# Last squares on VectorE, head transposes two steps later, a shorter Newton step in a two-block transformer kernel

## The chip, the cores and the metric

The kernel runs on one core of one Trainium2 chip. The core has five engines that work side by side, each from a queue of its own and in order: TensorE (PE, with PEld for its weight loads), VectorE (DVE), ScalarE (ACT), GpSimd (POOL) and SyncE (SP, which here only starts DMAs). The metric is device microseconds for one execution, the median of the timed runs.

## The reference

Two transformer blocks run one after the other on 256 tokens of width 2048, all in float32. The first has stick-breaking attention, sparse attention and a gated feed-forward; it ends in an RMS norm. The second, in which most of the change lies, has eight "Fox" heads (softmax attention with a forget bias) and eight "NSA" heads, which sum a compressed, a selected and a window branch, then a SwiGLU feed-forward:

```python
def _rms_norm(x, g):
    xf = x.astype(jnp.float32)
    y = xf * lax.rsqrt(jnp.mean(xf * xf, axis=-1, keepdims=True) + RMS_EPS)
    return (y * g.astype(jnp.float32)).astype(x.dtype)

def second_block(x, ...):
    h = _rms_norm(x, attn_norm[l])
    x = x + _hybrid_mixer(h, ...)     # o_fox and o_nsa, concatenated, @ w_out
    h = _rms_norm(x, ffn_norm[l])
    x = x + _swiglu(h, w_gate[l], w_up[l], w_down[l])

# in a head
    p = _masked_softmax(s, mask)      # exp(s - max) / sum
    o = jnp.einsum("bhqk,bkhd->bqhd", p, v)
```

With 256 tokens, all key blocks are selected and the window covers everything, so the kernel computes two softmax branches of 384 masked columns (128 for the first 128 queries, 256 for the others) in each NSA head, and one in each Fox head.

## The kernel before

**Main products.** Activations lie with features on partitions and tokens on the free axis. All weights are streamed: a piece of 128 rows by up to 1024 columns comes by DMA (`raw`), ACT rounds it into a high part (`wh`, L303), and DVE takes the difference as a low part (`wl`, L306). Each product is done as several passes over high and low parts (L344 to L365) into PSUM pool `pg` of four buffers. `run` goes over a list of items; before the products of one piece it emits the splitting of the piece three further on (`AHEAD`), so `wh` and `wl` (four buffers each) can run up to three pieces ahead of PE. A piece of two 128-row slices by 512 columns is 2.56 us of PE.

**Side work.** Attention heads and norms are generators in the list `active`. `spent` adds up the columns of the products emitted, and every 1.27 us of them (`TICK`) `tick` moves each generator to its next `yield`. So the place of side work in each engine's queue is fixed by counting ticks; the schedule is manual, and each engine takes its instructions in the order in which they were emitted. `wait(n)` lets n ticks go by. `drain(gens)` ticks until the named generators are done, with no main products between; a group's `pre` runs such a drain, after the splitting for its first piece was emitted. Tiles of one tag share a number of buffers; a new tile's first writer waits until all readers of the buffer's last tile are done. The small PSUM tiles (`psm`) come from `pm`, with four buffers, for scores, transposes, outputs and norm sums alike.

**Heads.** `nsa_head` (L1537): scores 1; scores 2 and the softmax of branch 1; then that of branch 2; each softmax writes p (tag `t2`, two buffers in the pool `mixt`) by L821 on DVE and its exponential on ACT (L210). Then both are scaled (L837 on DVE), `wait(W)` with W = 3, six transposes on PE (L843) into two `psm` tiles, copies to SBUF (L447 on ACT or L449 on DVE, by turns), `wait(W)`, and the products with V (L680). The output is split by L683 (ACT) and L685 (DVE), and that frees its `psm` tile. `nsa_chain` starts a head every 7 ticks (`seq`). `fox_head` (L1619) is the same with one p, a head every 5 ticks, and starts when the NSA heads are done. `drain([gens["fox"]])` stands as `pre` ahead of the second half of the output projection, which needs the Fox outputs.

**Norms.** `x_out` (L1106) runs for each of 16 feature tiles k: high part (ACT), low part (L1113, DVE), square (ACT, tile `sq` of two buffers), and the add of the square to the running sum (L1118, POOL). The first block's last down projection has two sums, the output projection of the second block one. A product with ones (L1303 and L1304, or L1190) sums over partitions, and `rsqrt_of` (L493) makes the reciprocal root by Ln and Exp and one Newton step on DVE. It is called five times: ahead of both mixers and both feed-forwards, and once for the norm between the blocks.

Of the kernel before, what the change touches and what calls it, by code (L numbers as in the profile page):

```python
# [12 lines left out]
OP = mybir.AluOpType  # L13
# [13 lines left out]
W = 3  # L27
# [97 lines left out]
def kernel(ctx: ExitStack, tc: tile.TileContext, t):  # L125
    nc = tc.nc
    out = t["out"]
# [76 lines left out]
    def lut(func, **kw):  # L204

        if func in (AF.Exp, AF.Ln):
            ln_exp()
        else:
            tables[0] = func
        nc.scalar.activation(func=func, **kw)  # L210
# [16 lines left out]
    def wait(n):  # L227
        for _ in range(n):
            yield
# [263 lines left out]
    def rsqrt_of(out_, src, inv_n, w):  # L493

        r0 = tmp.tile([128, T], F32, name="r0", tag="r0", bufs=1)[:, :w]
        m = tmp.tile([128, T], F32, name="mm", tag="mm", bufs=1)[:, :w]
        lut(out=r0, in_=src, func=AF.Ln, scale=inv_n, bias=epsc)
        lut(out=r0, in_=r0, func=AF.Exp, scale=-0.5)
        nc.vector.tensor_scalar(out=m, in0=src, scalar1=inv_n, scalar2=EPS, op0=OP.mult, op1=OP.add)
        nc.vector.tensor_mul(out=m, in0=m, in1=r0)  # L500
        nc.vector.tensor_mul(out=m, in0=m, in1=r0)
        nc.vector.tensor_scalar(out=m, in0=m, scalar1=-0.5, scalar2=1.5, op0=OP.mult, op1=OP.add)
        nc.vector.tensor_mul(out=out_, in0=r0, in1=m)

    def ident_rows(off):
        return lambda k: off + k
# [55 lines left out]
    def first_norm():  # L562
        rsqrt_of(rb, sqs[2][:, :T], 1.0 / D, T)
        keep_warm(WARM)
        h_scale(0)
# [498 lines left out]
    def xk(k):  # L1064
        return P["x"][k // 8][:, k % 8, :]
# [40 lines left out]
    def x_out(k, g_ap, pair, accs):  # L1106

        x = xk(k)
        hi, lo = pair(k)
        yield  # L1110
        nc.scalar.activation(out=hi, in_=x, func=AF.Identity, scale=g_ap)
        yield
        nc.vector.scalar_tensor_tensor(out=lo, in0=x, scalar=g_ap, in1=hi.bitcast(F32), op0=OP.mult, op1=OP.subtract)  # L1113
        for acc, sc in accs:
            sq = acc if k == 0 else P["late"].tile([128, T], F32, name="sq", tag="sq")
            nc.scalar.activation(out=sq, in_=x, func=AF.Square, scale=1.0 if sc is None else sc)
            if k:
                nc.gpsimd.tensor_tensor(out=acc, in0=acc, in1=sq, op=OP.add)  # L1118

    ssq = {}  # L1120

# [415 lines left out]
    def nsa_head(h):  # L1537
        g, qh = h // 4, R["qn"][:, h, :]
        sd = R["t"].tile([128, 384], F32, name="t1", tag="t1")
        nc.scalar.activation(out=sd, in_=C["dist"], func=AF.Copy, scale=2.0 ** -(h + 1))  # L1540
        yield
        S1 = scores(qh, R["kv"][:, 4 + g, :])
        yield
        S2 = scores(qh, R["kv"][:, 6 + g, :])
        p1, st1 = yield from softmax(S1, sd, R["t"])
        p2, st2 = yield from softmax(S2, sd, R["t"])
        for i, (p, st) in enumerate(((p1, st1), (p2, st2))):
            nc.vector.reciprocal(out=st[:, 0:2], in_=st[:, 4:6])
            nc.vector.tensor_mul(out=st[:, 0:2], in0=st[:, 0:2], in1=R["gat"][:, 1 + i, h, :])
            scale_rows(p, st[:, 0:2])  # L1550
        yield from wait(W)
        PT1 = transpose_p(p1)
        PT2 = transpose_p(p2)
        yield
        pT = []
        for PT in (PT1, PT2):
            x = R["t"].tile([128, 384], F32, name="t3", tag="t3", bufs=3)
            copy(x, PT[:, :384])
            pT.append(x)
        yield from wait(W)  # L1560
        j = h // 2
        vc = R["vcT"][32 * j:32 * j + 32, 128 * (h % 2):128 * (h % 2) + 128]
        yield from av_out(pT, [(R["vsw"], 128 * g), (R["vsw"], 256 + 128 * g)], oN(), h,
                          extra=(vc, R["pcT"][32 * j:32 * j + 32, :]))
# [54 lines left out]
    def fox_head(h):  # L1619
        cb = R["t"].tile([128, T], F32, name="cb", tag="cb")  # L1620
        s = R["scr"][h:h + 1, :]
        nc.scalar.dma_start(out=cb, in_=bass.AP(tensor=s.tensor, offset=s.offset, ap=[[0, 128], [1, T]]))
        yield
        yield
        cm = R["t"].tile([128, 384], F32, name="t1", tag="t1")
        nc.gpsimd.tensor_tensor(out=cm[:, 0:128], in0=cb[:, 0:128], in1=R["negc"][:, 0, 0:128], op=OP.add)
        nc.gpsimd.tensor_tensor(out=cm[:, 128:384], in0=cb, in1=R["negc"][:, 1, :], op=OP.add)
        S = scores(R["qf"][:, h, :], R["kf"][:, h, :])
        yield
        p, st = yield from softmax(S, cm, R["t"], R["cq"][:, :, h])  # L1630
        nc.vector.reciprocal(out=st[:, 0:2], in_=st[:, 4:6])
        scale_rows(p, st[:, 0:2])
        yield from wait(W)
        PT = transpose_p(p)
        yield
        pT = R["t"].tile([128, 384], F32, name="t3", tag="t3", bufs=3)
        copy(pT, PT[:, :384])
        yield from wait(W)
        yield from av_out(pT, [(R["vf"], 128 * h)], oF(), h)
# [125 lines left out]
```

## Time and profile before

| | |
|---|---|
| median of 3 runs | 2741.2 us (2741.12 to 2746.78) |
| profiled execution | 2742.96 us, of which the span 2741.2 us |
| PE busy | 2681.7 us, 98% |
| PE weight loads | 2344.1 us, 86% |
| DVE busy | 1961.9 us, 72% |
| ACT busy | 1353.8 us, 49% |
| POOL busy | 498.2 us, 18% |
| mean granted TensorE clock | 0.995 |

The span runs from the first to the last instruction. Times in rows are microseconds from its start. The second block's mixer lies at about 1558 to 2010.

### The profile page before, as it was taken

The page shows a single profiled execution, that of the slowest core. Times are in us where ns is not written, and L with a number is a line of the kernel's source. Part 1 is how long each engine was busy: PE and PEld are TensorE (multiplying, and loading weights), DVE is VectorE, ACT ScalarE, POOL GpSimd, SP SyncE. Part 2 cuts the span into 40 slices and gives each one's busy share as a digit, 9 for nine tenths or more (in the row PEclk, how much of TensorE's full clock was granted, in tenths as well). Part 3 has the DMA queues.
Part 4 walks back from the last instruction along what each step waited for, and adds up shares of the span by engine and source line. Part 5 has one row for each costly group of instructions (what it writes and reads, how often), then busy time and mean ns, then how long its engine had stood idle before and what let it go on. Part 6 is the DMA issues. An engine that isn't in the chain of part 4 may idle for free. (4 is left out here: it accounts for less than half of the span.)

```text
span 2741.2 us, 42225 instructions
## 1 busy us (share of the span) xinstructions
PE 2681.7 (98%) x16017; PEld 2344.1 (86%) x16017; DVE 1961.9 (72%) x2843; ACT 1353.8 (49%) x2022; POOL 498.2 (18%) x469
## 2 busy tenths in 40 slices
PE   8989999899999999999999999999999999999999
PEld 6879997788878888888888878888888888888888
DVE  8899877988877886556666756767876665556655
ACT  5544553444446555335555535555554554344543
POOL 0444310310512010000102301102222220012210
PEclk9999999999999999999999999999999999999999
DMA  9888757889876885566665675444566666666664
GB/s 358 263 273 305 231 191 226 268 292 321 303 246 198 300 300 186 185 194 190 193 189 187 194 218 158 152 131 154 169 187 194 190 190 192 189 189 191 191 196 144
DMA packets 303820, 591.16 MB, mean 216 GB/s; under 512 B 20980, under 2 KB 61020, under 8 KB 303486
## 3 DMA queue, kind: packets, MB, share of 16 engines
q1 hardware_dynamic: 299990, 583.61, 66.1%
q10 hardware_dynamic: 3626, 4.85, 0.8%
q8 instruction: 126, 2.06, 0.3%
q14 instruction: 78, 0.64, 0.1%
HBM read 582.54 MB, written 5.78 MB: 215 GB/s over the span
## 5 line engine op out<-in xcount | busy, mean ns | idle before, releaser
L348 PE MATMUL pg<-ring,wh 128*128 128x512 f32 x5408 | 1904.4, 393 | 1.1 <-DVE ring L1174 0.9
L306 DVE TENSOR_TENSOR wl<-raw,wh 128x1024 fp32r<-128x1024 f32 (+2 forms) x908 | 1141.1, 1269 | 616.9 <-ACT wh L303 606.1
L347 PE MATMUL pg<-ring,wl 128*128 128x256 f32 x5408 | 1524.0, 282 | 6.8 <-DVE wl L306 4.9
L303 ACT ACTIVATE wh<-raw 128x1024 fp32r<-128x1024 f32 (+2 forms) x908 | 928.9, 1039 | 878.2 <-PE pg L348 646.6
L348 PEld LDWEIGHTS pg<-ring,wh 128*128 128x128 f32 x5408 | 1019.4, 188 | 216.3 <-DVE ring L1174 3.3
L347 PEld LDWEIGHTS pg<-ring,wl 128*128 128x128 f32 x5408 | 1018.1, 188 | 36.0 <-issue 10.0
L482 POOL TENSOR_TENSOR ring<-gy,ring 128x256 fp32r<-128x256 f32 x88 | 110.2, 1262 | 749.4 <-ACT ring L480 749.4
L350 PE MATMUL pg<-ring,wh 128*128 128x256 f32 x672 | 190.5, 284 | 8.1 <-DVE ring L456 3.1
L352 PE MATMUL pg<-ring,wl 128*128 128x256 f32 x672 | 188.2, 280 | 6.2 <-DVE wl L306 6.1
L351 PE MATMUL pg<-ring,wh 128*128 128x256 f32 x672 | 188.8, 281 | 0.1
L344 PE MATMUL pg<-ring,wh 128*128 128x512 f32 x352 | 142.3, 404 | 5.3 <-DVE ring L456 2.0
L350 PEld LDWEIGHTS pg<-ring,wh 128*128 128x128 f32 x672 | 127.0, 189 | 11.5 <-DVE ring L456 3.4
L314 DVE CUSTOM_DVE_ANT_0 raw<-raw,cb,mod 128x1024 f32<-128x1024 f32 x96 | 135.3, 1409 | 1.2 <-DMA raw<-in_w_adaT 0.8
L352 PEld LDWEIGHTS pg<-ring,wl 128*128 128x128 f32 x672 | 126.9, 189 | 7.9 <-DVE wl L306 7.8
L314 DVE CUSTOM_DVE_ANT_0 raw<-raw,cb,vec 128x1024 f32<-128x1024 f32 x96 | 130.0, 1354 | 1.5 <-DMA cb<-cdram 1.5
L351 PEld LDWEIGHTS pg<-ring,wh 128*128 128x128 f32 x672 | 126.8, 189 | 0.9 <-DVE ring L600 0.3
L467 POOL TENSOR_TENSOR ring<-pt,ring 128x256 f32<-128x256 f32 x76 | 87.2, 1149 | 191.1 <-ACT pt L466 191.0
L1240 POOL TENSOR_TENSOR gy<-ga,rb 128x256 f32<-128x256 f32 x44 | 52.5, 1202 | 325.2 <-ACT ga L210 325.2
L345 PE MATMUL pg<-ring,wl 128*128 128x256 f32 x352 | 98.8, 281 | 0.0
L363 PE MATMUL pg<-wh,ring 128*128 128x512 f32 (+3 forms) x240 | 85.2, 355 | 0.0
L364 PE MATMUL pg<-wl,ring 128*128 128x512 f32 (+3 forms) x240 | 80.6, 336 | 0.3 <-DVE wl L306 0.3
L365 PE MATMUL pg<-wh,ring 128*128 128x512 f32 (+3 forms) x240 | 80.6, 336 | 0.0
(292 smaller groups left out, 2424.2 us busy)
## 6 DMA issues: line engine op xcount, KB each, us to landing
raw<-in_w_in SPq DMA_DIRECT2D x241, 512.0 KB, 4.7
raw<-in_w_adaT SPq DMA_DIRECT2D x192, 512.0 KB, 5.4
raw<-in_w_gate SPq DMA_DIRECT2D x176, 512.0 KB, 4.2
raw<-in_w_up SPq DMA_DIRECT2D x176, 512.0 KB, 4.2
raw<-in_w_down SPq DMA_DIRECT2D x176, 512.0 KB, 4.6
raw<-in_w_out SPq DMA_DIRECT2D x64, 512.0 KB, 5.7
raw<-in_w_o_sb SPq DMA_DIRECT2D x16, 512.0 KB, 5.1
raw<-in_w_o_dsa SPq DMA_DIRECT2D x16, 512.0 KB, 6.0
```

Of the source, the lines that this page charges most:

```text
L303: nc.scalar.activation(out=hi, in_=src, func=AF.Copy)
L306: nc.vector.tensor_sub(out=lo, in0=src, in1=hi.bitcast(F32))
L314: nc.vector.tensor_tensor_reduce(out=r, in0=r, in1=P["cb"][:, RAW * half:RAW * half + RAW], scale=1.0, scalar=below, op0=OP.mult, op1=OP.a ...
L344: nc.tensor.matmul(g.ps[f], hi[:, fs], both, start=True, stop=False)
L345: nc.tensor.matmul(ps, lo[:, fs], xh, start=False, stop=False)
L347: nc.tensor.matmul(ps, lo[:, fs], xh, start=False, stop=False)
L348: nc.tensor.matmul(g.ps[f], hi[:, fs], both, start=False, stop=stop)
L350: nc.tensor.matmul(ps, hi[:, fs], xh, start=start, stop=False)
L351: nc.tensor.matmul(ps, hi[:, fs], xl, start=False, stop=False)
L352: nc.tensor.matmul(ps, lo[:, fs], xh, start=False, stop=stop)
L467: nc.gpsimd.tensor_tensor(out=y, in0=x, in1=y, op=OP.add)
L482: nc.gpsimd.tensor_tensor(out=lo, in0=src, in1=hi.bitcast(F32), op=OP.subtract)
```

## The change

It has three parts. In `rsqrt_of` the Newton step after its first product is done by two `scalar_tensor_tensor` instructions instead of a product, a scale-and-add and a product: m(-0.5)r0, then (m + 1.5)r0. In `x_out` the adds of squares for k of 12 and more run on VectorE instead of GpSimd. In `nsa_head` and `fox_head` five ticks instead of three lie between the scaling of the probabilities and their transposes; `ds_head` of the first block keeps three.

```diff
@@ -498,9 +498,8 @@
         lut(out=r0, in_=r0, func=AF.Exp, scale=-0.5)
         nc.vector.tensor_scalar(out=m, in0=src, scalar1=inv_n, scalar2=EPS, op0=OP.mult, op1=OP.add)
         nc.vector.tensor_mul(out=m, in0=m, in1=r0)
-        nc.vector.tensor_mul(out=m, in0=m, in1=r0)
-        nc.vector.tensor_scalar(out=m, in0=m, scalar1=-0.5, scalar2=1.5, op0=OP.mult, op1=OP.add)
-        nc.vector.tensor_mul(out=out_, in0=r0, in1=m)
+        nc.vector.scalar_tensor_tensor(out=m, in0=m, scalar=-0.5, in1=r0, op0=OP.mult, op1=OP.mult)
+        nc.vector.scalar_tensor_tensor(out=out_, in0=m, scalar=1.5, in1=r0, op0=OP.add, op1=OP.mult)
@@ -1115,7 +1114,8 @@
             if k:
-                nc.gpsimd.tensor_tensor(out=acc, in0=acc, in1=sq, op=OP.add)
+                eng = nc.vector if k >= 12 else nc.gpsimd
+                eng.tensor_tensor(out=acc, in0=acc, in1=sq, op=OP.add)
@@ -1548,7 +1548,7 @@
             scale_rows(p, st[:, 0:2])
-        yield from wait(W)
+        yield from wait(W + 2)
         PT1 = transpose_p(p1)
         PT2 = transpose_p(p2)
@@ -1630,7 +1630,7 @@
         scale_rows(p, st[:, 0:2])
-        yield from wait(W)
+        yield from wait(W + 2)
         PT = transpose_p(p)
```

## Rows read from the trace of the kernel before

**Rows 1.** Page, part 1: busy us (share of span) and instructions of each engine.

```profile
PE 2681.7 (98%) x16017; PEld 2344.1 (86%) x16017; DVE 1961.9 (72%) x2843; ACT 1353.8 (49%) x2022; POOL 498.2 (18%) x469
```

**Rows 2.** Who waited for whom (total us, times, longest): PE, whole span; DVE, 1745 to 1960.

```profile
PE pm L843 <- DVE t L837: 6.1, 6, 2.2
...
PE pg L344 <- DVE ring L1174: 0.9, 1, 0.9
...
DVE t L821 <- PE pm L843: 1.4, 3, 0.7
```

**Rows 3.** Stretches: length; PE, PEld, DVE, ACT, POOL busy (instructions); PE clock; DMA.

```profile
1568.00:1573.00 5.00, 4.94 (x17) 3.96 (x18) 3.79 (x6) 3.75 (x5) 0.69 (x2) 0.66 0.74 239
...
1923.00:1928.00 5.00, 5.00 (x22) 4.32 (x21) 4.77 (x11) 1.64 (x4) 0.54 (x2) 0.66 0.95 325
...
1758.00:1763.00 5.00, 2.73 (x15) 1.83 (x15) 4.86 (x11) 3.28 (x6) 2.54 (x2) 1.00 0.36 107
```

**Rows 4.** Timeline of PE: start, us, instruction, [idle before it <- releaser]; transposes of two heads.

```profile
1761.54 0.70 PE L843 MATMUL pm<-con,t 128*128 128x128 f32 x3 [2.13 <-DVE t L837]
...
1922.48 0.70 PE L843 MATMUL pm<-con,t 128*128 128x128 f32 x3 [2.23 <-DVE t L837]
```

**Rows 5.** Timelines of DVE and PE around transposes of NSA heads 0, 1 and 2.

```profile
1763.46 0.28 DVE L821 CUSTOM_DVE_ANT_0 t<-pm,t 128x128 f32<-128x128 f32 x1
...
1777.19 0.42 DVE L685 TENSOR_TENSOR ring<-pm,ring 128x256 fp32r<-128x256 f32 x1
...
1777.75 0.46 PE L812 MATMUL pm<-ring 128*128 128x128 f32 x2 [0.21 <-DVE ring L685]
...
1792.62 0.82 PE L843 MATMUL pm<-con,t 128*128 128x128 f32 x6
...
1793.14 0.29 DVE L821 CUSTOM_DVE_ANT_0 t<-pm,t 128x128 f32<-128x128 f32 x1 [0.36 <-PE pm L843]
...
1793.36 0.42 DVE L821 CUSTOM_DVE_ANT_0 t<-pm,t 128x256 f32<-128x256 f32 x1
```

**Rows 6.** PE, end of Fox: main products of 1951.5 to 1956.47 by line, then timeline.

```profile
L348 PE MATMUL pg<-ring,wh 128*128 128x512 f32 x14 | 4.9, 393 | 0.0
...
1957.26 0.70 PE L843 MATMUL pm<-con,t 128*128 128x128 f32 x3
1958.74 0.94 PE L680 MATMUL pm<-t,ringv 128*128 128x128 f32 x6 [0.79 <-ACT t L447]
```

**Rows 7.** Timeline of DVE at the end of Fox.

```profile
1955.47 0.55 DVE L449 COPY t<-pm 128x384 f32<-128x384 f32 x1
...
1956.72 0.15 DVE L1631 RECIPROCAL st<-st 128x2 f32<-128x2 f32 x1
1956.91 0.55 DVE L837 TENSOR_SCALAR t<-t,st 128x128 f32<-128x128 f32 x2
1957.38 1.66 DVE L1128 TENSOR_TENSOR ring<-pg,ring 128x256 f32<-128x256 f32 x4
1958.96 2.35 DVE L306 TENSOR_TENSOR wl<-raw,wh 128x1024 fp32r<-128x1024 f32 x2
```

**Rows 8.** Last squares of the first block: DVE, 1557 to 1569, by line; timelines of POOL and PE.

```profile
L306 DVE TENSOR_TENSOR wl<-raw,wh 128x1024 fp32r<-128x1024 f32 x4 | 5.3, 1358 | 2.4 <-ACT wh L303 2.4
...
L1113 DVE SCALAR_TENSOR_TENSOR ring<-ring,gain 128x256 fp32r<-128x256 f32 x4 | 3.5, 914 | 0.0
...
1562.48 6.21 POOL L1118 TENSOR_TENSOR ssq<-ssq,sq 128x256 f32<-128x256 f32 x6 [1.69 <-ACT sq L1116]
...
1568.06 0.70 PE L1303 MATMUL pm<-ssq,ones 128*128 128x256 f32 x2 [1.81 <-POOL ssq L1118]
```

**Rows 9.** DVE: Newton step of the first feed-forward's norm; L1219 of the whole span by line.

```profile
817.28 0.42 DVE L501 TENSOR_TENSOR mm<-mm,r 128x256 f32<-128x256 f32 x1
817.74 0.29 DVE L502 TENSOR_SCALAR mm<-mm 128x256 f32<-128x256 f32 x1
...
L1219 DVE SCALAR_TENSOR_TENSOR gy<-ga,vec,gy 128x256 f32<-128x256 f32 x44 | 21.0, 477 | 0.0
```

## The prediction

> **What bounds the kernel now.** I read the page first: TensorE (PE) is busy for 2681.7 of 2741.2 us, so every other engine matters only where it makes PE wait [rows 1]. About 59.5 us of idle PE are left, and the list of waits says to whom they belong. The change can reach only a few of them. The largest line that it aims at is the wait of the heads' transposes (L843) for the scaled probabilities (L837): 6.1 us in six times over the whole run [rows 2]. The timeline of PE places them: two long ones in the second block, at 1761.54 (2.13 us, first NSA head) and at 1922.48 (2.23 us, fourth Fox head) [rows 4]. The other edit aims at the sums of squares ahead of the last norm of the first block: PE waits 1.81 us for POOL at 1568.06 [rows 8].
>
> An idle stretch can cost a second time. After the wait at 1922.48 the granted clock has a mean of 0.66 over 1923 to 1928, that is, 3.4 us at the lower of the two levels (1.2 instead of 2.4 GHz), which costs 5 x 0.34 = 1.7 us of PE work; the same after 1568. After the wait at 1761.54, ahead of which three transposes ran, the clock stayed at 1.00 [rows 3].
>
> **Newton step.** `rsqrt_of` runs five times. Behind its first product a product, a scale-and-add and a product go out; two `scalar_tensor_tensor` come in. On VectorE (DVE) the product takes 0.42 us, the scale-and-add 0.29, with 0.04 between them; a `scalar_tensor_tensor` of 128x256 takes 0.477 [rows 9]. So 0.42+0.29+0.42+2 x 0.04 = 1.21 us become 2 x 0.477+0.04 = 0.99: 0.22 us a call. It counts where PE waits at the end of the chain, which is so at the norm of the first feed-forward (0.9 us for L1174) [rows 2], and I assume it for the very first norm too. The other three have no waiter. Gain **0.5 us** (bounds 0 and 0.7).
>
> **Squares on DVE.** Eight adds (k = 12 to 15, two sums) leave POOL, where the last six took 6.21 us, and go to DVE, at 0.42 us and a start each 0.46 [rows 8, 9]. DVE was full there: in 1557 to 1569 its four L306 have a mean of 1.358 us and its four L1113 of 0.914 [rows 8], beside 1.18 [rows 7] and 0.477 [rows 9] where POOL is idle. Without POOL's adds DVE gets back 4 x 0.18 + 4 x 0.44 = 2.5 us, and takes on 8 x 0.46 = 3.7. It is then 1.2 us later at the end of the second sum; the first sum, for which PE waits, is ready an add and its gap sooner than that, some 0.4 to 0.7 us later than now. So the wait isn't removed; the engine that is late changes from POOL to DVE. I take **+0.4 us**; the bounds are -3.5 (the wait and its slow clock gone) and +1.5. The second use, ahead of the last feed-forward, lies where PE has no wait; four adds on a DVE that is as full there I put at **+0.35 us** (0 to 1).
>
> The Trainium skill ("SBUF — State Buffer", section "SBUF: two separate sides") says that a port pair shared by GpSimd and VectorE is an exclusive lock, held for a whole instruction. The rows agree in kind (L1113 doubles); by the rule all of POOL's 6.2 us could have been blocked DVE time, the sums would end before PE comes, and the total would be that of the third rival.
>
> **Transposes two steps later: what goes.** A step (tick) is 1.27 us of main products, here 8 matmuls. The scaling of p2 of NSA head 0 is done at 1761.5 [rows 4]; PE would now come to it behind the scores of head 1, two ticks and one norm sum, at about 1762. The wait for L837 is gone, but the second half meets the new wait described next, since DVE writes the next head's p1 only at 1763.46 [rows 5]. PE passes that place some 1.5 us earlier than now: gain **1.5 us** (0 to 2.4). At Fox head 3 PE goes on to main products whose operands lie ready, and comes to the transposes 4 ticks later (2 for the later start of Fox, 2 of its own): gain 2.23 + 1.7 for the clock = **3.9 us** (2.2 to 3.9). The 0.21 us of the scores at 1777.75 go too [rows 5]: **0.2**.
>
> **What comes in, first: PSUM and p buffers of the NSA heads.** An NSA head has two probability tiles, and the tag `t2` has two buffers. Heads start 7 ticks apart. Numbered from head h's start, head h+1 has its scores 1 at tick 9, scores 2 and the write of its p1 (L821) at tick 10, p2 at tick 12. Before, the transposes of head h stand in tick 10, ahead of that L821; L821 needs the buffer that the first three of them read. The trace shows this link: L821 at 1793.14 waits for L843 and starts 0.52 us behind its start at 1792.62 [rows 5], one of three such waits [rows 2]. Now the transposes stand in tick 12, so DVE reaches L821 first and always waits. That alone holds up DVE (about 3 us each) and, behind it, the next L306 and on ACT the exponentials; both engines run up to three weight pieces (7.7 us of PE) ahead, so I put that at 0. But `pm` has four PSUM buffers. At tick 12 five are wanted: the output of head h-1 (freed by L685 in tick 11, which now queues behind the held L821), scores 1 and scores 2 of h+1, and the two tiles of the transposes. That four is the limit, the trace shows too: scores at 1777.75 wait for L685, and start 0.14 us behind its end [rows 5]. So PE does the first three transposes, then waits until L821 has read scores 1: 0.52 to its start, 0.64 for its two parts (1793.14 to 1793.78), 0.14 to PE, less 0.41 (half of 0.82) for the three transposes = 0.89 us. Heads 1 to 6: 6 x 0.89 = **+5.3 us** (0 to 9; more where DVE is late as well).
>
> **Second: the tail of Fox.** Fox starts when NSA has ended, 2 ticks later than now, and each Fox head is 2 ticks longer, so the last ends 4 ticks later. That end is not free: ahead of the second half of the output projection `drain` runs the rest with no main products between. From the transposes of head 6 to its products with V are 4 ticks, 16 pairs of matmuls; only 14 pairs run, so the drain begins in that fourth tick [rows 6]. At present it holds products of head 6, transposes of head 7 (1957.26), one copy on ACT and products of head 7, which end at 1959.68: a wait of 0.79 us [rows 6]. Four ticks later the drain begins with the transposes of head 6, and the scaling of head 7 falls into it as well. On DVE that scaling now stands behind two weight pieces, which are queued before the drain begins: four L1128 (1.66 us), two L306 (2.35), then reciprocal and scaling (0.74), the low part of head 5 (0.42) and the copy of head 6, which falls to DVE (0.55) [rows 5, 7]. From 1956.6, PE's last main product, that is 5.7 us less some 0.5 for L1128 that start sooner: the copy is ready at about 1961.9. Behind it on PE: products of head 6 (0.94, as those of head 7), from transposes to products of head 7 1.48, products 0.94 = 3.36, so the end is at about 1965.3; half a microsecond, partly for transposes that stood ahead of the drain, is saved: 1964.8 instead of 1959.68. **+5.1 us** (1 to 7), and **+1.7** for the clock, since a PE idle for 4 us in one piece is longer than either of the waits that brought it down (0 to 1.7).
>
> **Sum.** -0.5 +0.4 +0.35 -1.5 -3.9 -0.2 +5.3 +5.1 +1.7 = +6.75 us. The profiled execution spans 2741.2 us and took 2742.96 in all; the median of the timed runs is 2741.2, so the sum is added to that: **2747.9 us**, 0.25% slower. Differences under 0.2% (5.5 us) can hardly be told from none.
>
> **Rivals.**
> 1. The buffers don't bind: another `pm` buffer is free at tick 12, or DVE frees one in time. For it: one single wait for `pm` by that name is in the rows. Against: the count of five. 2747.9 - 5.3 = 2742.6, within 0.2%.
> 2. The tail is covered: the last head's scaling gets ahead of the weight pieces, because one more tick fits before the drain. 2747.9 - 6.8 = 2741.1, within.
> 3. The port goes free with POOL's adds and DVE has both sums ready before 1566.25, where PE now begins to wait: 2747.9 - 3.9 = 2744.0, within. Against: my count of DVE's queue.
> 4. The other side: DVE's queue isn't held to the order of the program, so that neither the held L821 nor the two L306 stand in front of what PE needs. It decides in the drain, from the point that L837 of the last head starts before the two L306. All of 12.1 us comes back: 2735.8, faster. Against: at present L306 runs at 1958.96 [rows 7] exactly where the program has it, ahead of the low parts of heads 6 and 7.
> 5. DVE's hold of 3 us in each head uses up the three pieces of lead: some 2 us of PE wait on L306 in 4 or 5 heads, +9: 2757, slower. Against: DVE waits now and then for PE there, which is slack.
>
> **How the numbers follow.** Forecast 0.42; rivals 0.12, 0.12, 0.12, 0.12, 0.10. The forecast's own range is 2743 to 2752; two thirds of it (0.28) is over the bound of 2746.7. Slower 0.28 + 0.10 = 0.38. Within: 0.14 + 0.36 + 0.03 from rival 4, whose 2735.8 lies on the bound = 0.53. Faster 0.09. The range 2737 to 2753 leaves out most of rivals 4 and 5.
>
> **What would show it.** PE rows of L843 that wait for DVE L821 between the third and the fourth transpose in six NSA heads, 0.9 us each; no wait at 1761 and 1922; at the end of Fox a wait of 4 us or more for L449 behind two L306, and a clock of about 0.66 behind it; L1303 waiting for DVE instead of POOL. No wait at the fourth transpose would break the second largest step, a drain as short as now the largest.

## The result, and the profile after

The changed kernel takes 2767.8 us (median of five runs; before, timed beside it, 2741.25). These medians have a ratio of 1.0097; estimated from all the runs it is 1.0064, with a 95% interval of 1.0039 to 1.009. The kernel is slower, for which the prediction had a chance of 0.38, beside 0.53 for a difference within 0.2%; by the medians it is 26.6 us slower instead of 6.7, and outside the range. The five times stand in two groups, and the median falls in the upper one: 2755.77 and 2755.97, and 2767.8, 2769.43 and 2769.74. The profiled execution is one of the longer (2769.43, span 2767.6). Both groups have to be explained: 14.7 us of loss in the shorter runs, and some 13 more in the longer ones.

The page of after, busy time of each engine; to be read beside [rows 1]:

```profile
PE 2698.4 (97%) x16017; PEld 2347.2 (85%) x16017; DVE 1955.3 (71%) x2850; ACT 1351.6 (49%) x2022; POOL 488.4 (18%) x457
```

PE's busy time has grown by 16.7 us for the same 16017 matmuls. So a good part of the loss is no wait at all: the matmuls themselves took longer. The rest should be in the list of PE's waits (who waited for whom: total us, times, longest), which answers to [rows 2]:

```profile
PE pm L842 <- DVE st L820: 5.4, 7, 1.0
...
PE pm L679 <- DVE t L449: 4.8, 2, 4.4
PE pg L344 <- ACT wh L303: 3.3, 1, 3.3
...
PE pg L344 <- DVE ring L1128: 2.8, 2, 1.8
...
PE pm L842 <- DVE t L836: 1.6, 2, 1.0
...
PE pm L1303 <- DVE ssq L1118: 1.2, 1, 1.2
```

(From `rsqrt_of` to `x_out` line numbers are one lower than before: L843 is now L842, L821 L820, L680 L679.) The wait for the scaling (L837, now L836) has fallen from 6.1 us to 1.6; the bubbles at L842 are there, the drain's wait for the copy L449 too, and there is one line that the prediction did not have at this place: PE waits 3.3 us for a high part, `wh`.

The timeline of PE in after shows where these stand (start, us, instruction, [idle before it <- releaser]):

```profile
1568.43 0.70 PE L1303 MATMUL pm<-ssq,ones 128*128 128x256 f32 x2 [1.21 <-DVE ssq L1118]
...
1762.88 0.55 PE L842 MATMUL pm<-con,t 128*128 128x128 f32 x3 [0.99 <-DVE st L820]
...
1778.96 0.55 PE L842 MATMUL pm<-con,t 128*128 128x128 f32 x3 [0.74 <-DVE st L820]
...
1914.22 0.47 PE L344 MATMUL pg<-ring,wh 128*128 128x512 f32 x1 [1.83 <-DVE ring L1128]
...
1930.82 0.76 PE L344 MATMUL pg<-ring,wh 128*128 128x512 f32 x1 [3.31 <-ACT wh L303]
1933.39 0.76 PE L344 MATMUL pg<-ring,wh 128*128 128x512 f32 x1 [0.96 <-DVE ring L1128]
...
1968.08 1.65 PE L679 MATMUL pm<-t,ringv 128*128 128x128 f32 x6 [4.37 <-DVE t L449]
...
1970.95 1.65 PE L679 MATMUL pm<-t,ringv 128*128 128x128 f32 x6 [0.58 <-ACT t L447]
```

Around the end of the waits at 1930.8 and 1968.1 the granted clock falls to the lower level, for 6.8 us each, as two stretches of after show (columns as in [rows 3]; a mean of 0.52 over 7 us):

```profile
1930.00:1937.00 7.00, 5.23 (x18) 4.41 (x19) 6.86 (x13) 1.11 (x2) 1.14 (x2) 0.52 0.25 82
1968.00:1975.00 7.00, 6.34 (x24) 5.60 (x25) 0.88 (x3) 1.26 (x3) 0.00 (x0) 0.52 0.26 95
```

**The 13 us without a wait.** From 2050 to 2650, in the last feed-forward, PE has no wait in the list of either trace and the clock stands at 1.00. By line, PE's groups there, first before, then after:

```profile
L348 PE MATMUL pg<-ring,wh 128*128 128x512 f32 x1632 | 570.0, 392 | 0.0
L347 PE MATMUL pg<-ring,wl 128*128 128x256 f32 x1633 | 455.3, 279 | 0.0
```

```profile
L348 PE MATMUL pg<-ring,wh 128*128 128x512 f32 x1605 | 571.0, 397 | 0.0
L347 PE MATMUL pg<-ring,wl 128*128 128x256 f32 x1604 | 446.1, 278 | 0.0
```

In the same 600 us after gets through 27 pairs fewer. A pair of L347 and L348 takes, as a median from start to start, 346.7 ns in the one and 353.3 in the other: the same instructions run in one of two **cadences**. Over some 2000 such pairs from 2011 to the end that is 13.2 us, the distance between the two groups of times.

**The account.** Both kernels issue the same 15,120 main products (L344 to L365) in the same order. I laid the start times of the two traces side by side and summed, by stretch, by how much each gap between neighbours had grown:

| stretch (us of before) | after minus before, us | forecast |
|---|---|---|
| 1565 to 1575: first block's sums | -2.4, of which -1.6 is the slow clock of [rows 3], which after's trace doesn't have | +0.4 |
| 1750 to 1880: NSA heads | +4.0 | +3.6 |
| 1880 to 1945: Fox heads | +4.1 | -3.9 |
| 1945 to 1961: end of Fox, drain | +7.1 | +6.8 |
| 2011 to the end: cadence | +13.4 | none |

With -0.8 for the sums (the part that isn't the clock) the first four give +14.4: 2741.2 + 14.4 = 2755.6, the shorter group; with the cadence 2769.0, the longer one.

### The profile page after: what moved, and what is told of

Its sections match the earlier page's. It is cut to its first block, busy times and chain, and to the rows that moved or that the text cites. A ratio compares the mean times of both kernels' runs of the same rounds, so it can differ in the third digit from the quotient of the medians.

```text
span 2767.6 us, 42224 instructions
## 1 busy us (share of the span) xinstructions
PE 2698.4 (97%) x16017; PEld 2347.2 (85%) x16017; DVE 1955.3 (71%) x2850; ACT 1351.6 (49%) x2022; POOL 488.4 (18%) x457
## 4 chain that ended last, share of the span: by engine, by line
PE 69%; DVE 4%; DMA 2%; ACT 2%; issue 1%; POOL 1%; SPq 0%; ACTq 0%; DVEq 0%
PE pg L348 39%; PE pg L347 20%; PE pg L344 3%; DVE wl L306 2%; PE pg L345 1%; PE pm L679 1%; ACT wh L303 1%; PE pg L363 1%; PE pg L364 1%; PE pg L365 1%; DMA raw<-in_w_out 1%; PE pm L1475 1%; DVE raw L314 1%; DMA raw<-in_w_o_dsa 0%; POOL ring L482 0%
## 5 line engine op out<-in xcount | busy, mean ns | idle before, releaser
L348 PE MATMUL pg<-ring,wh 128*128 128x512 f32 x5408 | 1913.9, 395 | 1.1 <-DVE ring L1174 0.9
L306 DVE TENSOR_TENSOR wl<-raw,wh 128x1024 fp32r<-128x1024 f32 (+2 forms) x908 | 1137.8, 1266 | 622.6 <-ACT wh L303 612.6
L347 PE MATMUL pg<-ring,wl 128*128 128x256 f32 x5408 | 1521.7, 281 | 7.2 <-DVE wl L306 6.0
L348 PEld LDWEIGHTS pg<-ring,wh 128*128 128x128 f32 x5408 | 1015.9, 188 | 228.6 <-DVE ring L1174 3.3
L347 PEld LDWEIGHTS pg<-ring,wl 128*128 128x128 f32 x5408 | 1015.1, 188 | 36.5 <-issue 10.1
L344 PE MATMUL pg<-ring,wh 128*128 128x512 f32 x352 | 143.4, 407 | 9.2 <-ACT wh L303 3.3
L345 PE MATMUL pg<-ring,wl 128*128 128x256 f32 x352 | 99.4, 282 | 0.0
L365 PE MATMUL pg<-wh,ring 128*128 128x512 f32 (+3 forms) x240 | 81.0, 338 | 0.0
```

The costliest lines, as they stand in the source:

```text
L306: nc.vector.tensor_sub(out=lo, in0=src, in1=hi.bitcast(F32))
L344: nc.tensor.matmul(g.ps[f], hi[:, fs], both, start=True, stop=False)
L345: nc.tensor.matmul(ps, lo[:, fs], xh, start=False, stop=False)
L347: nc.tensor.matmul(ps, lo[:, fs], xh, start=False, stop=False)
L348: nc.tensor.matmul(g.ps[f], hi[:, fs], both, start=False, stop=stop)
```

## The experiments

The kernels were timed in five series, with before among them in each. Times below are medians, with the ratio to before and its 95% interval; where times stand in two groups, "lower" is the mean of the lower one, and the times of the other are called long. Before's lower group lay at 2740.1 to 2742.0 in the five series. "Laid side by side" is the account above, from 1750 to 1961. The edits are shown in excerpts.

**Each part alone.** Four kernels, each with one part of the diff: the Newton step, the squares, `wait(W + 2)` in `nsa_head`, `wait(W + 2)` in `fox_head`.

> The kernel before with the three-instruction Newton step alone. Forecast's step: -0.5 us (2740.7), at most -0.7. Rival: the step is too small to be seen, but where PE stands ahead of a long run of main products decides between two cadences of that run (346.7 and 353.3 ns a pair in the traces of before and after), so single executions could come out some 13 us longer without any wait in the list; then a part of the executions lies near 2754.

> The kernel before with the last squares on VectorE alone. Forecast's step: +0.4 and +0.35, 2741.9; after's own trace has a wait of 1.21 us for VectorE at the first sum instead of 1.81 for POOL and no stretch at the lower clock behind it, so nearer to 2739 to 2740 (-0.6 for the wait, -1.7 for the clock). Theory of the cadence: the product with ones ahead of the last feed-forward now waits for VectorE for some 0.07 us, and that puts the 726 us behind it into the slower cadence in some executions: two groups of times, about 2740 and 2753.5. Rival: the long cadence comes from the heads' part, and these times stay in one group within 2 us.

> The kernel before with the two steps more in the NSA heads alone. Forecast's steps: head 0 and scores -1.7, six bubbles of 0.89 us +5.3 (in after's trace 0.74, so +4.4), and Fox starts two ticks later, for which nothing but the end of Fox is priced: its drain begins two ticks earlier in the heads' own count, worth 0 to +4. Sum 2743 to 2748. Rival: the holds on VectorE and ScalarE stop the supply of weight pieces, PE waits for wh or wl at 1900 to 1940, and the time goes beyond 2750. By the cadence theory no second group 13 us higher, as its product with ones doesn't wait.

> The kernel before with the two steps more in the Fox heads alone. Forecast: -3.9 at head 3, and about half of the drain's 6.8 us or less, since the last head ends 2 ticks later instead of 4: 2738 to 2743. Rival (holds between VectorE and ScalarE): waits for wh of over 2 us at 1910 to 1940, with the lower clock behind them, 2745 or more. By the cadence theory no second group 13 us higher.

Measured: Newton 2741.96 (ratio 1.0006, 0.9987 to 1.0025), squares 2746.44 (1.0012, 0.9991 to 1.0032), NSA 2756.36 (1.0049, 1.0029 to 1.007), Fox 2741.81 (0.9992, 0.9974 to 1.001). All four, and before itself, have long executions: 3 of 10, 5 of 10, 5 of 8, 1 of 10, and 6 of 29. My expectation that only the squares would bring a second group is wrong; before has it as well. The lower groups are 2741.0, 2741.7, 2748.7 and 2741.9, against 2742.0 of before. The groups aren't sharp: one time of the Newton step (2747.7, counted as long) and two of before (2748.1 and 2748.9, not counted) lie between them, and NSA's spread from 2747.5 to 2765.2. So NSA costs some 7 us, and nothing else costs or gives much by itself. In a_squares the long cadence stood in the first block's feed-forward, not in the last one. PE by line from 900 to 1500, and its wait at the first sum (L1304 there):

```profile
L348 PE MATMUL pg<-ring,wh 128*128 128x512 f32 x1605 | 571.0, 397 | 0.0
```

```profile
1581.29 0.70 PE L1304 MATMUL pm<-ssq,ones 128*128 128x256 f32 x2 [1.22 <-DVE ssq L1119]
```

Laid side by side, NSA alone costs 8.5 us (3.9 to 1880, 4.6 in Fox that starts two ticks later and in its drain), Fox alone 0.5: it wins 3.6 before 1920 and loses 3.9 behind, at a new wait of its own, in the timeline of PE:

```profile
1922.78 1.04 PE L680 MATMUL pm<-t,ringv 128*128 128x128 f32 x6 [2.71 <-DVE t L449]
```

**Both heads together.** The two `wait(W + 2)`, Newton step and squares as before.

> Both heads' parts together, Newton step and squares as before. With the main products of two traces laid side by side in their order, from the first transposes of the NSA heads to the end of Fox's drain, NSA alone costs some 8.7 us, Fox alone 0.5 and the whole change 15.2. If the parts add up: 9 us longer there than before. If Fox, longer by two steps in each head and started two steps later, meets another step of the side work (PE's wait of 3.31 us for wh at 1930.8 in after, which neither part alone has): 15 us, with that wait in the list. Single executions may lie 13 us higher where one of the two long feed-forwards runs in the slower cadence.

2758.57 us (1.0065, 1.005 to 1.0081; four runs, all in one group). Laid side by side 14.6 us, where the parts alone sum to 9.0, with the wait that neither part has:

```profile
1929.81 0.77 PE L344 MATMUL pg<-ring,wh 128*128 128x512 f32 x1 [2.96 <-ACT wh L303]
```

**Is it Fox's place?** Fox alone with its two steps, and a start two ticks later by a wait of its own (with the three small products that the part on the cadence explains):

```diff
+        yield from wait(2)
         yield from seq([fox_late(h) for h in range(8)], 5)
```

> The two steps more in Fox alone, and Fox started two ticks later by a wait of its own; NSA heads as before; the three small products against the slower cadence. If the place in the count of ticks makes the collision, Fox looks as in the whole change: a wait of about 3 us for wh near 1925, 4.37 us for L449 in the drain, 11 us more than before from 1880 to 1961, in all about 2754 (before with the three products: 2743.5). If it needs the NSA heads' holds, the wait for wh is missing and it is 3 to 5 us less.

2755.13 us. Laid side by side 10.9 us, all of it behind 1920, though the NSA heads are those of before. The waits are those of after:

```profile
1929.25 0.76 PE L344 MATMUL pg<-ring,wh 128*128 128x512 f32 x1 [3.32 <-ACT wh L303]
...
1966.02 1.65 PE L680 MATMUL pm<-t,ringv 128*128 128x128 f32 x6 [4.37 <-DVE t L449]
```

So the NSA heads' holds aren't needed for this wait. Heads longer by two ticks that also start two ticks later make it; two more ticks alone (a_fox), or the later start alone (a_nsa), don't.

**What holds `wh` back.** In after ScalarE and VectorE wait for each other by turns ahead of 1930.8. Their timelines, ScalarE first:

```profile
1920.17 0.69 ACT L1375 ACTIVATE hm<-pm,epsc 128x512 f32<-128x512 f32 x1 [4.41 <-DVE ring L1386]
...
1922.09 1.05 ACT L303 ACTIVATE wh<-raw 128x1024 fp32r<-128x1024 f32 x1
1926.02 0.40 ACT L210 ACTIVATE t<-t,st 128x128 f32<-128x128 f32 x1 [2.89 <-DVE st L826]
...
1928.74 1.99 ACT L303 ACTIVATE wh<-raw 128x1024 fp32r<-128x1024 f32 x2
```

```profile
1916.23 2.89 DVE L306 TENSOR_TENSOR wl<-raw,wh 128x1024 fp32r<-128x1024 f32 x2
...
1919.38 0.67 DVE L1386 TENSOR_TENSOR ring<-ring,hm 128x512 f32<-128x512 f32 x1
1923.16 1.46 DVE L306 TENSOR_TENSOR wl<-raw,wh 128x1024 fp32r<-128x1024 f32 x1 [3.11 <-ACT wh L303]
...
1925.83 0.16 DVE L826 TENSOR_TENSOR st<-cq,st 128x2 f32<-128x2 f32 x1
```

L1375 writes `hm`, which has one buffer, and waits for its last reader L1386, which stands on VectorE behind two L306. The next `wh` stands behind L1375 on ScalarE; L306 waits for it on VectorE, and a head's L826 behind that L306; the head's exponential waits for L826 on ScalarE, with the next `wh` behind it. When PE comes, its lead of three pieces is used up: 24 pairs, 8.3 us at 346.7 ns a pair. (The 2.56 us a piece given above, and the prediction's 7.7 us, are the program's own count of columns.) So I gave `hm` a second buffer in the changed kernel:

```diff
-        m = R["t"].tile([128, 512], F32, name="hm", tag="hm", bufs=1)[:, :w]
+        m = R["t"].tile([128, 512], F32, name="hm", tag="hm", bufs=2)[:, :w]
```

> The whole change, with a second buffer for hm of the heads' norms (the tile ct of the forget bias shares a buffer with cb to make room). In after ScalarE's L1375 at 1920.17 waits 4.41 us for VectorE's L1386, the reader of hm's only buffer; VectorE then waits 3.11 us for wh, ScalarE 2.89 us for st, and PE 3.31 us for wh at 1930.82. If that one buffer is the head of the chain, the wait for wh goes with most of the slow clock behind it: 4 to 7 us less than after in that stretch. Rival: the weight pieces queued on VectorE (L306) hold the chain by themselves, and a wait for wh of 2 to 3 us stays.

The times fell apart (2744.41 to 2773.42; lower 2745.4, five of eight long, one of them twice so), so the trace decides. PE's waits:

```profile
1922.00 0.47 PE L344 MATMUL pg<-ring,wh 128*128 128x512 f32 x1 [1.35 <-ACT wh L303]
...
1924.42 0.47 PE L344 MATMUL pg<-ring,wh 128*128 128x512 f32 x1 [1.50 <-DVE ring L1128]
```

The wait for `wh` falls from 3.31 to 1.35, no slow clock follows (1.00 from 1922 to 1929), and from 1880 to 1945 4.5 us are back. The buffer is one link of the chain and not the whole of it: ScalarE still waits 4.87 us for L826 ahead of 1917.2.

**The bubbles of the NSA heads.** The changed kernel with four buffers for the heads' probabilities:

```diff
-        p = pool.tile([128, 384], F32, name="t2", tag="t2")
+        p = pool.tile([128, 384], F32, name="t2", tag="t2", bufs=4 if pool is R.get("t") else 2)
```

> The whole change, with four buffers for the heads' probabilities t2 (ct and the compressed branch's scores share buffers with cb to make room). By the forecast's step the write of the next head's p1 is no longer held by the transposes, its scores' PSUM buffer comes free in time, and the seven waits between third and fourth transpose (0.99 and six of 0.74 us) are gone: 5.4 us less than after from 1755 to 1860. Rival: PSUM's four buffers are too few by themselves, and the waits stay at 0.7 or more for another releaser. Fox as in after: its wait for wh and its drain stay.

2748.47 us; 1.0026 (1.0003 to 1.0048) of before. PE's waits for VectorE at L842 from 1755 to 1880, seven in after, are one, head 0's:

```profile
PE pm L842 <- DVE st L820: 1.0, 1, 1.0
```

6.4 us are back in that stretch: the six bubbles (6 x 0.74 = 4.4) and what hung on them. Fox's waits stay as they were. The forecast's chain of causes, L820 held by the buffer of `t2` and the scores' PSUM tile held by L820, is thus shown.

**The drain.** The changed kernel, with Fox's drain emitted ahead of the splitting of the next piece (`early` is set for the first group of the second half alone):

```diff
+            if g is not None and g.done == 0 and g.pre and g.early:
+                g.pre()
+                g.pre = None
             split_to(*(whalf[min(pos + a, len(whalf) - 1)] for a in AHEAD))
```

> The whole change, but ahead of the second half of the output projection the drain of Fox is emitted before the splitting of the next weight piece instead of behind it, so that the two L306 (2.35 us) stand behind the last head's scaling and the copy on VectorE. Forecast's step: those two are 2.35 of the 4.37 us of PE's wait for L449; the wait falls to about 2.0, with perhaps a shorter slow clock behind it: -2.4 to -4 us from 1956 to 1961 against after. Rival: the wait ends with something else (the exponentials on ScalarE, wh ahead of them), and falls by less than 1.

2750.64 us (1.0035, 1.0015 to 1.0055); lower 2749.5, beside 2754.7 of the changed kernel in the same series. VectorE's timeline in after's drain has the last head's scaling and the copy behind two L306, and PE starts 0.05 us behind the copy's end (1968.03):

```profile
1964.23 2.35 DVE L306 TENSOR_TENSOR wl<-raw,wh 128x1024 fp32r<-128x1024 f32 x2
1966.49 0.16 DVE L1631 RECIPROCAL st<-st 128x2 f32<-128x2 f32 x1
1966.68 0.55 DVE L836 TENSOR_SCALAR t<-t,st 128x128 f32<-128x128 f32 x2
1967.15 0.42 DVE L684 TENSOR_TENSOR ring<-pm,ring 128x256 fp32r<-128x256 f32 x1
1967.48 0.55 DVE L449 COPY t<-pm 128x384 f32<-128x384 f32 x1
```

With L306 behind them PE's wait is 2.10 instead of 4.37, that is, 2.27 less for an L306 pair of 2.35, and the slow clock is gone in this execution (1.00 over 1963 to 1970):

```profile
1963.67 0.94 PE L682 MATMUL pm<-t,ringv 128*128 128x128 f32 x6 [2.10 <-DVE t L452]
...
1963.00:1970.00 7.00, 5.75 (x37) 5.09 (x38) 3.62 (x6) 3.79 (x6) 0.00 (x0) 1.00 0.01 2
```

**The cadence.** First the changed kernel again, and before with a small product 16 times in each long feed-forward:

```diff
+    def shake():
+        yield from wait(24)
+        for _ in range(16):
+            nc.tensor.matmul(psm()[:, 0:128], ones, C["ident"], start=True, stop=True)
+            yield from wait(32)
```

> The changed kernel itself again, beside the other kernels of this call, for its spread. If the longer of its two times (2769 beside 2756) is the slower cadence in one of the two long feed-forwards, struck anew in each execution, its times should again lie in groups some 13 us apart, the lowest near 2754, with before's own spread in the same groups from about 2737 on. If it belongs to the change, nearly all executions lie near 2768.

> The kernel before, with one more small product (128x128 by 128 columns, of which nothing is read) every 32 ticks, 16 times in each of the two long feed-forwards: some 0.2 to 0.3 us each, 32 of them, +7 to +10 us. Theory: the cadence is struck anew wherever the row of main products is interrupted, and kept until the next such place. Then in the trace the cadence changes at these products and nowhere between, a part of the pieces is slow, and the times lie closer together, without groups 13 us apart. Rival: an execution or a stretch of weights has its cadence for another reason (an address, a transfer), and the products change nothing in it: whole feed-forwards fast or slow as before.

The changed kernel: 2756.65 (1.0056, 1.0035 to 1.0077), with seven times at 2751.8 to 2757.3, four at 2766.2 to 2769.0 and one at 2777.8. Before, in that series: 8 of 35 at 2752 or more. With the small products all 12 times lie between 2745.3 and 2750.6, at 0.22 us for each product: no group 13 us higher. In the profiled execution the cadence was the faster one behind every one of them.

Then three such products only, at some 861, 1000 and 2037 us, in before, in the changed kernel and in a mended version (below).

> The kernel before with three small products (128x128 by 128 columns, nothing reads them; 0.22 us each): two in the first long feed-forward, at about 861 and 1000 us, one in the second, at about 2037. If the slower cadence ends at a product that doesn't wait, no execution has it for long: all times within some 6 us of 2741, none in the group at 2752 to 2759, in which some 8 of 35 of before lie. Rival: the cadence isn't touched by such a product, and about a fifth of the times lies 13 us higher as now.

> The whole change with the same three products. If the cadence alone makes the groups, all times lie in one group at 2752 to 2757, where without them 5 of 12 lay at 2766 to 2778; against the kernel before with the three products the whole change costs 12 to 15 us, made of NSA +4, the wait for wh and its slow clock, Fox's drain and the squares' -1. Rival: a second cause in the change; then a group near 2767 stays.

> Newton step, squares, four buffers for t2 and two steps more in NSA heads 0 to 6, with the three products. One group, at 2736 to 2742, 2 to 3 us below the kernel before with the three products: with the cadence out of the way the small gain can be told from none. Rival: the gain in the profile (-1.6 in the NSA heads, -0.9 at the first squares) is lost elsewhere, and the two lie within 1 us.

Medians 2743.49 (2739.14 to 2746.27), 2756.12 (2751.30 to 2759.37) and 2739.0 (2735.72 to 2745.69), 12 runs each, and no long one among them; before without them had 18 long ones of 35 in the same series. Over all kernels with such products it is 0 of 70 runs; before alone, over the five series, 36 of 137. With the cadence out of the way **the whole change costs 12.6 us** (2756.12 - 2743.49).

One trace shows the switch itself. In d_after_kick the weight load of the product with ones (L1196 there, L1190 before) waited for VectorE; 0.18 us lie between the starts of the two loads, in place of 0.12:

```profile
2021.38 0.19 PEld L348 LDWEIGHTS pg<-ring,wh 128*128 128x128 f32 x1
2021.56 0.36 PEld L1196 LDWEIGHTS pm<-ssq,ones 128*128 128x128 f32 x2
```

From there the main products ran in the slower cadence, until the small product at 2045.80 (in e_fox_late likewise from 896 to the small product at 1003). PE by line from 2023 to 2045, the small product, and PE by line from 2048 to 2070:

```profile
L348 PE MATMUL pg<-ring,wh 128*128 128x512 f32 x60 | 21.4, 397 | 0.0
...
2045.80 0.38 PE L1089 MATMUL pm<-con,ones 128*128 128x128 f32 x2
...
L348 PE MATMUL pg<-ring,wh 128*128 128x512 f32 x60 | 21.0, 392 | 0.0
```

**Do the squares bring it on?** The wait of that weight load is 61 to 68 ns in seven traces, all with the squares on VectorE; behind it the cadence is the slower one in three of the seven. In 13 traces without the wait it is the faster one every time. That the wait is the cause isn't shown by this: in ten of the 13 PE comes to the product in the slower cadence already, and leaves it in the faster one; of those that come in the faster cadence only three are without the wait. So I left the last norm's squares on GpSimd:

```diff
-                eng = nc.vector if k >= 12 else nc.gpsimd
+                eng = nc.vector if k >= 12 and len(accs) > 1 else nc.gpsimd
```

> The whole change, but the squares ahead of the last feed-forward stay on GpSimd; those of the first block's two sums move as in the change. In all traces so far with those squares on VectorE in which PE comes to that norm in the faster cadence, its weight load waits 61 to 68 ns for VectorE (five of five), and two of the five go on in the slower cadence for 739 us; of nine traces without that wait none does. Expected: no such wait (gap of 117 to 118 ns between the weight loads), the faster cadence behind it, and long times in about a fifth of the executions, as with before, instead of five of twelve. Rival: the stall isn't what sets the cadence, and five or more of twelve are long.

2764.23 us: seven of 12 long, not fewer; but before had 18 of 35 long in that series. The profiled execution has no such wait and the faster cadence behind 2036; but PE comes there in the slower cadence, in which four traces with the squares on VectorE have no wait either, so it says nothing of the squares. It is the first block's feed-forward that is slow there (837 to 1572). So squares or not, the slower cadence begins elsewhere too, and whether the change makes long executions more frequent is not settled.

**Everything taken away.** The changed kernel with three buffers for `t2`, two for `hm`, the early drain and the three small products:

> The whole change with what was taken away one at a time before, together: three buffers for t2, two for hm (ct, the compressed branch's scores and sums share buffers with cb), Fox's drain emitted ahead of the splitting, and the three small products. If these are the whole loss and independent: 2756.1 less 6.4 (NSA), 4.5 (wait for wh) and 5.2 (drain) = 2740.0, some 3 us below the kernel before with the three products (2743.5). Rival: taking them away together moves something else onto the path, and it stays above 2744.

2740.03 us (0.9993, 0.9979 to 1.0007), 2740.0 expected. Before's lower group lay at 2740.1 in that series, so what is back is about the loss. That the time came out to a tenth is luck: laid side by side, 13.2 of the 15.2 us that after loses are back. No wait for `wh` is left in the second block's mixer. Of the drain's wait 2.10 us are left, as in c_drain, but here the clock is at the lower level behind it for 6.8 us, and the drain still costs 4.9 us against before:

```profile
1952.00:1959.00 7.00, 6.14 (x24) 5.36 (x25) 2.12 (x4) 3.15 (x5) 0.00 (x0) 0.54 0.01 2
```

The NSA heads, 2.8 us shorter than before's, and the squares make up for it. So the named mechanisms account for most of the loss; that each gives back its share independently isn't shown.

**A better version.** From the parts: Newton step and squares as in the change, Fox as before, and NSA with four buffers for `t2` and

```diff
-        yield from wait(W)
+        yield from wait(W + 2 if h < 7 else W)
```

so that Fox starts when it started before. A first try had the Newton step, the squares and the two steps in Fox alone.

> Newton step, squares on VectorE and the two steps more in Fox alone; NSA heads as before. By the parts measured alone: squares -0.9 (without the slow clock at that place, which comes and goes), Fox 0.5 to the end of its drain, Newton 0 to -0.5: 0 to -1.5 us, within the measurement. If there is a cost in the parts together it should show as a new wait of PE between 1890 and 1960.

> Newton step and squares as in the change; four buffers for t2; two steps more in NSA heads 0 to 6 only, so that Fox starts where it started before; Fox heads as before. By the runs so far: NSA -2.4 us (head 0's wait halved, no bubbles), squares -0.9, Fox 0: about 3 us less than before with the cadence taken out. If the last NSA head or Fox's start is touched all the same, new waits show between 1880 and 1960 and eat it up.

The first (b_best) has Fox's 0.5 us of a_fox and nothing else new; its four times, 2753 to 2764, were all long, and the profiled one ran in the slower cadence in both feed-forwards. The second (c_best): 2740.98 (0.999, 0.9971 to 1.001), lower 2738.5 against 2742.0 of before; laid side by side -1.5 us. So without the small products it can't be told from before. With them (d_best_kick) it is 2739.0, 4.5 us under before with them (2743.49) and 17 under the changed kernel with them. The ratio of 0.9967 to before without them (0.9947 to 0.9988) holds the gain by the products too, since 18 of before's 35 were long.

## Why the prediction was off

**Newton step (-0.5).** Too small for the times: a_newton's lower group lies 1.0 us under before's, within their spread. The traces show it. The exchanged instructions take 0.89 us in a_newton (from 817.69) instead of 1.22 (from 817.28), so 0.33 a call where I had 0.22:

```profile
817.69 0.43 DVE L501 SCALAR_TENSOR_TENSOR mm<-mm,r 128x256 f32<-128x256 f32 x1
818.15 0.43 DVE L502 SCALAR_TENSOR_TENSOR rb<-mm,r 128x256 f32<-128x256 f32 x1
```

Laid side by side from 800 to 822.5, the main products gain 0.22 to 0.33 us on before in all twelve traces with the new step, and nothing in the seven without. At the very first norm PE's first main product starts 6.82 us behind the end of the step in a_newton, 6.83 in before, so there the 0.33 should count as well. This step was right.

**Squares (+0.4, +0.35).** The engine waited for changed as forecast, from POOL [rows 8] to VectorE; the size was wrong, and with it the sign: the wait fell from 1.81 to 1.21 us (1.22 in a_squares), where I had it rise. VectorE by line from 1557 to 1569 in after, then its last low parts in before:

```profile
L306 DVE TENSOR_TENSOR wl<-raw,wh 128x1024 fp32r<-128x1024 f32 x3 | 3.6, 1220 | 1.5 <-ACT wh L303 1.5
L1118 DVE TENSOR_TENSOR ssq<-ssq,sq 128x256 f32<-128x256 f32 x8 | 3.0, 417 | 0.0
L1112 DVE SCALAR_TENSOR_TENSOR ring<-ring,gain 128x256 fp32r<-128x256 f32 x4 | 1.9, 476 | 0.0
```

```profile
1564.72 2.70 DVE L1113 SCALAR_TENSOR_TENSOR ring<-ring,gain 128x256 fp32r<-128x256 f32 x3
```

VectorE got back about what I had counted: L1112 (L1113 in [rows 8]) is at 476 ns instead of 914, as I had assumed, and L306 at 1220 instead of 1358, where I had 1180. But the eight adds took 3.0 us, where I had 3.7, and I added VectorE's delay to the wrong moment. Before, its last low part ends at 1567.42, 0.64 us ahead of PE's product at 1568.06, which waited for POOL; I had counted from the latter.

The Trainium skill ("SBUF — State Buffer", section "SBUF: two separate sides") has the loser of the port pair that VectorE and GpSimd share blocked for a whole instruction. The rows agree in kind, but not with the prediction's reading that all of POOL's 6.2 us could have been blocked time: beside those six adds VectorE's two L306 took 2.89 us, in place of 2.35 [rows 7], and its three L1113 2.70, in place of some 1.4, together some 1.8 us more.

The slow clock behind this wait, a part of my lower bound, is no sure thing either: in a_newton the wait is the same 1.81 us, and the clock stayed up. The step came out between the forecast and the third rival: the wait did not go, but it shrank. The other use costs 0.07 us of stall instead of 0.35, in seven of eleven traces; behind three of the seven the slower cadence began.

**NSA heads (-1.5, -0.2, +5.3).** Right: the waits for the scaling at 1761.5 and for the scores at 1777.75 are gone, a bubble between the third and the fourth transpose stands in each of heads 0 to 6, 0.74 us where I had 0.89, and 0.99 at head 0. The sum is +4.0 instead of +3.6; b_t2 shows the cause. The first rival is out.

**Fox, head 3 (-3.9).** Here the prediction failed. The wait of 2.23 us for the scaling and its slow clock went as forecast: between the main products on either side after gains 4.4 us on before, 0.7 of them because the transposes now stand elsewhere. But I priced the removal and not the new place, where I had PE go on to "main products whose operands lie ready". I moved whole heads by up to four ticks against the norm of the next queries and keys, the weight pieces and the evacuations, and assumed that a lead of three pieces would cover it. It was used up within 12 us by turns of ScalarE and VectorE; PE waited 3.31 and 0.96 us, with 6.8 us at the lower clock level. +4.1 instead of -3.9 is 8 us, nearly all of the error in the shorter runs, and enough to put these (2755.9) above the range, too. The fifth rival had the mechanism (holds use up the lead) and nearly the time (2757), but on L306 in four or five NSA heads and not on `wh`, once, in Fox. There I had written of VectorE's waits as slack, and looked at neither the order on ScalarE nor the single buffer of `hm`.

**Tail of Fox (+5.1, +1.7).** Right in mechanism and sum: +7.1 instead of +6.8. In the sum two errors cancel: the lower clock level lasted 6.8 us, which costs up to 3.4 where I had 1.7, so that at least 3.7 are left for the wait, where I had 5.1. The wait is 4.37 us for L449 behind two L306, as the prediction named it, and c_drain shows the link. The second and fourth rivals are out.

**The cadence (not in the sum).** It makes the difference between 2755.9 and the median of 2767.8. Before's trace could have shown it: L348 takes 392 ns from 2050 to 2650 and 397 from 1962 to 2010, without a wait in either. And 2746.78 among three runs was a hint that executions of one kernel differ; I looked at waits only. The range, made of waits and clocks, was too narrow by this spread, which struck before itself in 36 of 137 runs.

## What to carry to other kernels

A step that is moved in a hand-made schedule needs a price at its new place, on every in-order queue there: follow the next two or three instructions of each engine, look for single buffers, and ask whether two engines will wait for each other by turns; a lead of a few pieces doesn't cover that. A wait that disappears with a small edit is half the answer. And before a change of half a per cent is believed, look whether the kernel's own times have groups: the counts of equal matmuls in equal stretches tell in which group a profile was taken.

## What the runs showed of the hardware

Pairs of float32 products (512 and 256 columns, each with its weight load) run at 346.7 or 353.3 ns a pair, at the same granted clock of 1.00. A row keeps its cadence for as long as 739 us; in the two long feed-forwards it changed at interruptions only: at a stall (the shortest 0.06 us) or at products of another kind (L344 and L345, or a product with ones). Behind a small product that didn't wait it was the faster one in all traces, and 0 of 70 runs with such products were long. Why there are two, and what decides at an interruption, no run here shows; before's share of long runs went from 2 of 23 to 18 of 35 between series. The drop of the granted clock behind a wait is not certain either: after 1.81 us of wait at the same product it came in before's trace and not in a_newton's, after 2.10 us in the drain in e_all's and not in c_drain's.
